# Three branch pairs of a recurrent stage: the wide form of a seven-product scheme in place of the narrow one

## The chip, the cores and the metric

The kernel runs on one core of a Trainium2 chip. The metric is device time in microseconds (us) of one execution, lower is better. The times before are those of three runs; the profile is of one more execution, taken by the hardware profiler.

## The reference

One hybrid decoder layer on 512 tokens of width 1024, in float32:

```python
f = swiglu(rms_norm(h, ...), ...);  h = h + 0.5 * rms_norm(f, ...)
u = rms_norm(h, mix_norm_pre);      proj = u @ w_in          # q, k, v, xr, yr, gl
attn_d = dilated_attention(q, k, v) @ w_attn_branch
rec    = rg_lru(conv4(xr)) * gelu(yr)                        # 1024 channels, 4 heads of 256
rec_d  = rec @ w_rec_branch
merged = sigmoid(gl)[0] * attn_d + sigmoid(gl)[1] * rec_d
h = h + rms_norm(merged @ w_out, ...)
f = swiglu(rms_norm(h, ...), ...);  h = h + 0.5 * rms_norm(f, ...)
```

The change touches `yr`, the "branch" of the recurrence: 1024 of the output columns of `w_in`, taken head by head as two blocks of 128 columns. For heads 0, 1 and 2 these products are computed by another sequence of instructions; what is computed is the same.

## The kernel before

**Precision.** Every float32 operand is kept as two parts, a high part rounded to the matmul's own format (fp32r) and a low part, the rest. A product is the sum of three matmuls: high weights with high input, high weights with low input, low weights with high input. `split` (L302, L303) makes the parts: ScalarE copies the high part, VectorE subtracts it to get the low one.

**Seven products for eight.** Two weight blocks of 128 columns ("g" and "u") and two halves of 256 tokens form a 2 x 2 product with 8 halves' products over 512 input rows each. The kernel uses a seven-product scheme: sums of weight blocks (`w_forms_within`, L704 on: additions L713 to L717 and four splits) and sums of input quarters (the forms `t`, made once for the whole stage) give products p1 to p7, and sums of these give the four outputs g[0], g[1], u[0], u[1] of 128 x 256. TensorE accumulates in PSUM tiles of 128 x 512 float32 ("acc", five buffers in turn, and "aux", three); a running sum goes from one buffer to another by a ScalarE copy, and the next product accumulates onto the copy.

There are two ways to run it:

- The **narrow** form, `seven_on` (L733): one product is, for each of four 128-row blocks of the input, three matmuls of 256 columns (`seventh`, L729 to L731), so 84 matmuls in a pair. It uses four "acc" buffers, half of each. Four results are moved with ScalarE copies of 256 columns (the copies b to y, z to c5, b to c6, b to v), two outputs are evicted by ScalarE and two by VectorE.
- The **wide** form, `seven_wide` (L762): high and low part of the input lie side by side, so one matmul of 512 columns (L779) multiplies the high weights with both, and one of 256 columns (L780) adds low weights times high input to the second half of the buffer. 56 matmuls in a pair. The two halves of a buffer are added only when a result leaves PSUM: `move` (L784) copies 512 columns, `fold` (L790, L791) is a ScalarE copy and a VectorE addition of 256 columns, `sum_of` (L797, L798) two VectorE additions. It uses five "acc" buffers, all of each.

The wide form is what the attention stage uses for its query and key pairs and for the four gate pairs, which end at about 600 us. The recurrent stage uses the narrow form for its four branch pairs, with the signs that the scheme leaves on u (`two_tiles`: scale -1 in the ScalarE eviction, a `scalar_tensor_tensor` on VectorE).

**The recurrent stage** (600 to 820 us) follows a list of steps:

```python
LRU_ORDER = (("branch", 0), ("branch", 1), ("conv", 0), ("branch", 2), ("gates", 0), ("conv", 1), ("branch", 3),
             ("gates", 1), ("conv", 2), ("gate1", 1), ("gates", 2), ("conv", 3), ("gate1", 2), ("gates", 3),
             ("gate1", 3))
```

`conv` is two blocks of 24 matmuls of 512 columns (L315 to L317) and, for each, a VectorE copy out of PSUM (L1559), a ScalarE scaling (L1560), three VectorE taps (L1562) and a split. `gates` multiplies the convolved columns ("rec", later "rb") with the gate weights of a head into "aux" and "acc" tiles; ScalarE applies the sigmoid (L1618) and `recur` runs the recurrence on ScalarE (L1629 to L1642, four activation tables) and VectorE (L1634 to L1647, with a scan). `gelus` (L1587) applies the GELU to the branch results of heads 0 and 1 after branch 1, and of heads 2 and 3 after branch 3. Each step's weights are split one step ahead.

**What sets the order.** Each engine runs its instructions in one order, which a planner writes when the program is built: it takes the program order, priorities (evictions are raised by `EVAC` = 200 places, weight preparation by `AHEAD` = 100) and its own cost estimates. So a change in one step can move instructions of other steps on an engine. TensorE, ScalarE (ACT) and VectorE (DVE) wait for each other by semaphores; the weights come as one stream of transfers on SyncE's queue (SP), and a few transfers on GpSimd's (POOL).

Of the kernel before, what the change touches and what calls it, by code (L numbers as in the profile page):

```python
# [12 lines left out]
AF = mybir.ActivationFunctionType  # L13
ALU = mybir.AluOpType
# [169 lines left out]
def hybrid_layer(ctx: ExitStack, tc: tile.TileContext, xT: bass.AP, xN: bass.AP, wst: bass.AP,  # L184
                 first: bass.AP, rows: bass.AP, consts: bass.AP, bias: bass.AP, out: bass.AP):
    nc = tc.nc
    DVE, ACT, PE = nc.vector, nc.scalar, nc.tensor
# [71 lines left out]
    def fetch(key, slot=None, ahead=0):  # L259

        with tc.high_priority(offset=ahead if slot else state["ahead"]):
            src = raw_of(key)
            w = src.shape[-1]
            t = slot() if slot else w8() if w > 512 else w4()
            split(t[:, 0, :w], t[:, 1, :w], src)
            return t[:, 0, :w], t[:, 1, :w]
# [38 lines left out]
    def acc_ps():  # L305
        return psum.tile([P, T], F32, name="acc", tag="acc", bufs=5)
# [4 lines left out]
    def tmp(name):  # L311
        return tpool.tile([P, T], F32, name=name, tag="t")
# [17 lines left out]
    def gemm(ps, wt, x, sl=slice(0, T), ks=None):  # L330
        n = x.n
        a, b = k128(wt[0], n), k128(wt[1], n)
        for k in ks or range(n):
            mm3(ps, a[:, k, :], b[:, k, :], x.hi[k][:, sl], x.lo[k][:, sl], k == 0, k == n - 1)
# [17 lines left out]
    HALVES = (slice(0, HB), slice(HB, T))  # L352
# [380 lines left out]
    def seven_on(t, w, g0, g1, u0, u1):  # L733

        b, z, y, v = (acc_ps()[:, :HB] for _ in range(4))

        def copy(ps, dst=None):
            if dst is None:  # L740
                dst = tpool.tile([P, HB], F32, name="c", tag="c", bufs=CB)
            with tc.high_priority(offset=EVAC):
                ACT.activation(dst, ps, AF.Copy)  # L743
            return dst

        seventh(t, w, "p1", b, True)
        copy(b, y)
        seventh(t, w, "p5", z, True)
        c5 = copy(z)
        seventh(t, w, "p6", b, False)  # L750
        c6 = copy(b)
        seventh(t, w, "p2", y, False)
        g0(y)
        seventh(t, w, "p7", b, False)
        copy(b, v)
        u1(b, c5)
        seventh(t, w, "p3", z, False)
        g1(z, c6)
        seventh(t, w, "p4", v, False)
        u0(v)  # L760

    def seven_wide(t, w, g, u, seen=lambda ap: ap, then=lambda: None):  # L762


        b, z, y, v, o = (acc_ps() for _ in range(5))

        def two(ps):
            return ps[:, :HB], ps[:, HB:]

        def product(p, ps, start):  # L770
            at = t[p].at
            part, cross = ps.rearrange("q (s c) -> q s c", s=2), two(ps)[1]
            if len(at(0, 0).shape) == 3:
                part = ps.rearrange("q (s b t) -> q s b t", s=2, b=2)
                cross = cross.rearrange("q (b t) -> q b t", b=2)
            for k in range(4):
                ks = slice(k * P, (k + 1) * P)
                wh, wl = w[p][:, 0, ks], w[p][:, 1, ks]
                PE.matmul(part, wh, at(BOTH, k), start=start and k == 0, stop=False, skip_group_check=True)  # L779
                PE.matmul(cross, wl, at(0, k), start=False, stop=k == 3, skip_group_check=True)  # L780

        def move(dst, src):
            with tc.high_priority(offset=EVAC):
                return ACT.activation(dst, src, AF.Copy).ins  # L784

        def fold(ps, dst=None):
            out = tpool.tile([P, HB], F32, name="c", tag="c", bufs=CB) if dst is None else dst
            x, y_ = two(ps) if dst is None else map(seen, two(ps))
            with tc.high_priority(offset=EVAC):
                ACT.activation(out, x, AF.Copy)  # L790
                DVE.tensor_add(out, y_, out)  # L791
            return out

        def sum_of(dst, ps, c):
            x, y_ = two(ps)
            with tc.high_priority(offset=EVAC):
                DVE.tensor_add(c, x, c)  # L797
                DVE.tensor_add(dst, seen(y_), seen(c))  # L798

        product("p1", b, True)  # L800
        move(y, b)
        product("p5", z, True)
        c5 = fold(z)
        product("p6", y, False)
        move(v, y)
        c6 = fold(y)
        product("p2", b, False)
        fold(b, g[0])
        product("p7", v, False)
        moved = move(o, v)  # L810
        sum_of(u[1], v, c5)
        with tc.issue_after(moved):
            then()
        product("p3", z, False)
        sum_of(g[1], z, c6)
        product("p4", o, False)
        fold(o, u[0])

    def seven(t, w, z, g, u):

# [297 lines left out]
    for k in range(KC):  # L1118
        wh, wl, raw = wts[k]
        if k == 0:  # L1120
# [3 lines left out]
            for sl in HALVES:  # L1124
                tail = ACT.activation(wh[:, sl], raw[:, sl], AF.Copy).ins
            DVE.scalar_tensor_tensor(u1.lo[0], z, col("g1a", 0), u1.hi[0].bitcast(F32),
                                     op0=ALU.mult, op1=ALU.subtract)
# [69 lines left out]
    with ExitStack() as mx:  # L1197
# [38 lines left out]
        def values_two(steps, then):  # L1236
# [78 lines left out]
            for j in range(2):  # L1315
# [4 lines left out]
        t, steps = forms_of(lambda i, j: Form(lambda s, k: um_t[2 * i + k // 2][:, s, k % 2, HALVES[j]]),  # L1320
                            apool, False, rec_half)
# [38 lines left out]
        scale = -1.0 / math.sqrt(P)  # L1360
# [128 lines left out]
        for c in range(0, KC, 2):  # L1489
            g, u = tmp("g"), tmp("u")  # L1490
            seven_wide(t, pair_of(("pair", 52 + c, 53 + c)), [g[:, h] for h in HALVES], [u[:, h] for h in HALVES],
                       then=gate)
# [3 lines left out]
        for c in range(KC):  # L1496
            ps = acc_ps()
# [5 lines left out]
    with ExitStack() as mx:  # L1503
# [26 lines left out]
        def two_tiles(w, g, u):  # L1530

            lo, hi = HALVES

            def up(dst, ps, sign):
                with tc.high_priority(offset=EVAC):
                    ACT.activation(dst[:, lo], ps, AF.Copy, scale=sign)

            def g1(ps, c):
                with tc.high_priority(offset=EVAC):
                    DVE.tensor_add(g[:, hi], ps, c)  # L1540

            def u1(ps, c):
                with tc.high_priority(offset=EVAC):
                    DVE.scalar_tensor_tensor(u[:, hi], ps, -1.0, c, op0=ALU.mult, op1=ALU.subtract)

            seven_on(t, w, lambda y: up(g, y, 1.0), g1, lambda v: up(u, v, -1.0), u1)
# [19 lines left out]
        gels, late = {}, []  # L1566

        def branch(hd):

            gels[hd] = []  # L1570
            if ("branch", hd) in PAIRED:
                w = paired.pop(("branch", hd))
                gels[hd] = [lpool.tile([P, T], F32, name="ge", tag="ge", bufs=8) for _ in range(2)]
                two_tiles(w, *gels[hd])
                return
            for c in (2 * hd, 2 * hd + 1):
                ps = acc_ps()
                gemm(ps, fetch(("in", 44 + c)), um)
                ge = lpool.tile([P, T], F32, name="ge", tag="ge", bufs=8)
                with tc.high_priority(offset=EVAC):  # L1580
                    DVE.tensor_copy(ge, ps)
                gels[hd].append(ge)
# [67 lines left out]
        for i, (what, hd) in enumerate(LRU_ORDER):  # L1650
# [9 lines left out]
            def then():  # L1660
                if i + 1 < len(LRU_ORDER):
                    prepare(LRU_ORDER[i + 1])
# [21 lines left out]
        for c in range(KC):  # L1684
            if c < 3:
                ps = pss[c]
            else:
                ps = acc_ps()
# [163 lines left out]
```

## Time and profile before

| | |
|---|---|
| median of 3 runs | 1212.2 us (1211.42 to 1212.27) |
| profiled execution | 1211.87 us, its span 1210.1 us |
| TensorE busy | 1199.2 us (99%) |
| VectorE busy | 1029.0 us (85%) |
| ScalarE busy | 832.4 us (69%) |
| mean granted TensorE clock | 0.998 |
| chain that ended last | TensorE 88%, VectorE 6%, ScalarE 3%, DMA 2% |

The span is the time from the first to the last instruction of the profile; the rest of the execution's time lies around it. Matmuls are pipelined: each row's duration is longer than the distance to the next start, and the distance is what a matmul costs in a stream. A row of a timeline shows start, duration, engine, line, operation, output and inputs, and in brackets the idle time before it with what ended it.

### The profile page before, as it was taken

The numbers are of one execution on the slowest core, as the hardware profiler recorded it, in microseconds if no ns is written. First come the engines' busy times: TensorE is split into PE (matmuls) and PEld (weight loads), VectorE is DVE, ScalarE is ACT, GpSimd is POOL, SyncE is SP. The second block draws the span as 40 slices with busy tenths as digits, with TensorE's granted clock in tenths as the row PEclk, the third lists the DMA queues.
The fourth block names the chain that finished last, engine by engine and source line by source line (L and its number), as shares of the span: only waits on it lengthen the run. The fifth ranks groups of instructions, "written<-read, shape, count | busy, mean of one in ns | idle before, by whom it ended". The sixth has DMA issues, their size and how long they took to land.

```text
span 1210.1 us, 18990 instructions
## 1 busy us (share of the span) xinstructions
PE 1199.2 (99%) x7306; PEld 1073.7 (89%) x7306; DVE 1029.0 (85%) x1608; ACT 832.4 (69%) x1447; POOL 26.1 (2%) x51
## 2 busy tenths in 40 slices
PE   9999999999999999999999999999999999999997
PEld 8899999999888889888889888888899999999996
DVE  7999888989689899999867899775799888888964
ACT  7566787887566576677735897834566687877763
POOL 0000000000011000000000000000100000000000
PEclk9999999999999999999999999999999999999999
DMA  7234343435625232222323432235443333343341
GB/s 266 87 97 140 114 138 116 133 118 157 243 109 145 70 114 79 88 96 70 126 77 111 145 135 87 87 110 186 148 137 117 123 121 125 121 130 115 123 174 70
DMA packets 45819, 149.78 MB, mean 124 GB/s; under 512 B 5152, under 2 KB 8608, under 8 KB 45728
## 3 DMA queue, kind: packets, MB, share of 16 engines
q1 hardware_dynamic: 38160, 131.09, 32.5%
q0 software_dynamic: 7280, 17.30, 4.2%
q8 instruction: 57, 0.93, 0.3%
q14 instruction: 34, 0.28, 0.1%
q10 hardware_dynamic: 288, 0.17, 0.0%
HBM read 138.06 MB, written 6.29 MB: 119 GB/s over the span
## 4 chain that ended last, share of the span: by engine, by line
PE 88%; DVE 6%; ACT 3%; DMA 2%; issue 1%; DVEq 0%
PE acc L729 9%; PE acc L731 9%; PE acc L730 9%; PE acc L779 8%; PE acc L315 7%; PE acc L317 7%; PE acc L316 7%; PE acc L780 4%; PE aux L1037 3%; PE aux L1038 3%; PE aux L1039 3%; DVE w L303 2%; DMA raw<-in_w 2%; PE acc L433 2%; PE acc L432 2%; PE acc L431 2%
## 5 line engine op out<-in xcount | busy, mean ns | idle before, releaser
L303 DVE TENSOR_TENSOR w<-raw,w 128x1024 fp32r<-128x1024 f32 (+1 forms) x272 | 297.4, 1098 | 36.2 <-ACT w L302 35.2
L302 ACT ACTIVATE w<-raw 128x1024 fp32r<-128x1024 f32 (+1 forms) x272 | 259.9, 959 | 89.4 <-PE acc L317 42.7
L729 PE MATMUL acc<-big,w 128*128 128x256 f32 x920 | 260.5, 283 | 0.0
L731 PE MATMUL acc<-big,w 128*128 128x256 f32 x920 | 260.3, 283 | 0.0
L730 PE MATMUL acc<-big,w 128*128 128x256 f32 x920 | 260.3, 283 | 0.0
L729 PEld LDWEIGHTS acc<-big,w 128*128 128x128 f32 x920 | 176.2, 192 | 1.9
L730 PEld LDWEIGHTS acc<-big,w 128*128 128x128 f32 x920 | 176.2, 192 | 1.7
L731 PEld LDWEIGHTS acc<-big,w 128*128 128x128 f32 x920 | 176.3, 192 | 0.0
L779 PE MATMUL acc<-big,w 128*128 128x512 f32 x320 | 115.0, 397 | 0.0
L780 PE MATMUL acc<-big,w 128*128 128x256 f32 x320 | 90.8, 284 | 0.0
L1037 PE MATMUL aux<-w,xf 128*128 128x512 f32 x224 | 87.5, 393 | 1.4 <-ACT w L302 0.9
L1038 PE MATMUL aux<-w,xf 128*128 128x512 f32 x224 | 87.5, 391 | 0.0
L1039 PE MATMUL aux<-w,xf 128*128 128x512 f32 x224 | 87.2, 389 | 0.0
L779 PEld LDWEIGHTS acc<-big,w 128*128 128x128 f32 x320 | 60.1, 188 | 13.2 <-ACT acc L784 0.2
L303 DVE TENSOR_TENSOR w<-s,w 128x1024 fp32r<-128x1024 f32 x51 | 62.2, 1220 | 3.2 <-ACT w L302 2.7
L780 PEld LDWEIGHTS acc<-big,w 128*128 128x128 f32 x320 | 60.4, 189 | 0.1
L315 PE MATMUL acc<-xf,w 128*128 128x512 f32 (+1 forms) x168 | 58.8, 352 | 0.0
L316 PE MATMUL acc<-xf,w 128*128 128x512 f32 (+1 forms) x168 | 58.6, 349 | 0.0
L317 PE MATMUL acc<-xf,w 128*128 128x512 f32 (+1 forms) x168 | 58.6, 349 | 0.0
L302 ACT ACTIVATE w<-s 128x1024 fp32r<-128x1024 f32 x51 | 53.9, 1057 | 6.2 <-PE acc L731 3.0
L743 ACT ACTIVATE c<-acc 128x256 f32<-128x256 f32 x74 | 28.2, 383 | 40.4 <-PE acc L731 40.2
L1037 PEld LDWEIGHTS aux<-w,xf 128*128 128x128 f32 x224 | 41.9, 188 | 10.2 <-ACT w L302 1.5
(453 smaller groups left out, 2934.2 us busy)
## 6 DMA issues: line engine op xcount, KB each, us to landing
raw<-in_w SPq DMA_DIRECT2D x232, 512.0 KB, 3.5
big<-xf POOLq DMA_DIRECT2D x6, 512.0 KB, 3.4
gains<-in_rows POOLq DMA_DIRECT2D x5, 512.0 KB, 5.4
h<-in_x SPq DMA_DIRECT2D x8, 256.0 KB, 5.3
h<-in_xn POOLq DMA_DIRECT2D x4, 512.0 KB, 6.0
kept_m<-h POOLq DMA_DIRECT2D x4, 512.0 KB, 2.9
vals<-in_w SPq DMA_DIRECT2D x4, 512.0 KB, 6.2
h<-kept_m POOLq DMA_DIRECT2D x4, 512.0 KB, 6.1
```

Source lines behind the costliest of these rows:

```text
L302: state["split"] = ACT.activation(dh, src, AF.Copy).ins
L303: state["low"] = DVE.tensor_sub(dl, src, dh.bitcast(F32)).ins
L315: PE.matmul(ps, wh, xh, start=first, stop=False)
L316: PE.matmul(ps, wh, xl, start=False, stop=False)
L317: PE.matmul(ps, wl, xh, start=False, stop=last)
L729: PE.matmul(ps, wh, xh, start=start and k == 0, stop=False, skip_group_check=True)
L730: PE.matmul(ps, wh, xl, start=False, stop=False, skip_group_check=True)
L731: PE.matmul(ps, wl, xh, start=False, stop=k == 3, skip_group_check=True)
L779: PE.matmul(part, wh, at(BOTH, k), start=start and k == 0, stop=False, skip_group_check=True)
L780: PE.matmul(cross, wl, at(0, k), start=False, stop=k == 3, skip_group_check=True)
L1037: PE.matmul(ps, xh, wh, start=first and j == 0, stop=False, skip_group_check=True)
L1038: PE.matmul(ps, xh, wl, start=False, stop=False, skip_group_check=True)
```

## The change

The branch pairs of heads 0, 1 and 2 call `seven_wide` in place of `two_tiles`; head 3 keeps the narrow form. `seven_wide` gets a parameter for the sign of u: with -1 the ScalarE copy of a fold and the last VectorE operation of `fold` and `sum_of` apply it. Every other call has sign 1 and the instructions it had.

```diff
-    def seven_wide(t, w, g, u, seen=lambda ap: ap, then=lambda: None):
+    def seven_wide(t, w, g, u, seen=lambda ap: ap, then=lambda: None, sign=1.0):
...
-        def fold(ps, dst=None):
+        def fold(ps, dst=None, sign=1.0):
...
-                ACT.activation(out, x, AF.Copy)
-                DVE.tensor_add(out, y_, out)
+                ACT.activation(out, x, AF.Copy, scale=sign)
+                if sign > 0:
+                    DVE.tensor_add(out, y_, out)
+                else:
+                    DVE.scalar_tensor_tensor(out, y_, sign, out, op0=ALU.mult, op1=ALU.add)
...
-        def sum_of(dst, ps, c):
+        def sum_of(dst, ps, c, sign=1.0):
...
-                DVE.tensor_add(dst, seen(y_), seen(c))
+                if sign > 0:
+                    DVE.tensor_add(dst, seen(y_), seen(c))
+                else:
+                    DVE.scalar_tensor_tensor(dst, y_, sign, c, op0=ALU.mult, op1=ALU.subtract)
...
-        sum_of(u[1], v, c5)
+        sum_of(u[1], v, c5, sign)
...
-        fold(o, u[0])
+        fold(o, u[0], sign)
...
-                two_tiles(w, *gels[hd])
+                if hd in (0, 1, 2):
+                    seven_wide(t, w, *([x[:, h] for h in HALVES] for x in gels[hd]), sign=-1.0)
+                else:
+                    two_tiles(w, *gels[hd])
```

## The prediction

> **What bounds the kernel now.** I read the page first (busy time and the chain), then the windows around the branch pairs, the waits of TensorE in the recurrent stage, and last the timelines of ScalarE (ACT) and VectorE (DVE) at each place where the changed order touches one of those waits. Two lines of the page say whose time this is:
>
> ```profile
> PE 1199.2 (99%) x7306; PEld 1073.7 (89%) x7306; DVE 1029.0 (85%) x1608; ACT 832.4 (69%) x1447; POOL 26.1 (2%) x51
> PEclk9999999999999999999999999999999999999999
> ```
>
> TensorE is busy 99% at full granted clock, so the change can only give time by shorter TensorE work or by removing TensorE's waits; it can take time only by making new ones. The second view is busy time by window: branch pair 0, pair 1, pair 2 (with four gate matmuls in it), the gates and convolution behind it, pair 3 (narrow in both kernels), then one wide pair of the gate stage, and last a stretch of a wide pair beside a fuller VectorE.
>
> ```profile
> 622.51:632.55 10.04, 10.04 (x85) 10.03 (x84) 6.04 (x8) 5.92 (x9) 0.00 (x0) 1.00 0.05 13
> 632.55:642.70 10.15, 10.15 (x86) 10.08 (x85) 6.35 (x9) 8.01 (x13) 0.00 (x0) 1.00 0.50 166
> 653.61:664.58 10.97, 10.97 (x89) 10.78 (x88) 10.25 (x15) 7.77 (x12) 0.00 (x0) 1.00 0.20 60
> 664.58:680.09 15.51, 15.51 (x70) 12.77 (x69) 10.50 (x14) 14.35 (x20) 0.00 (x0) 1.00 0.32 102
> 680.09:692.61 12.52, 11.02 (x88) 10.57 (x87) 12.52 (x20) 9.34 (x16) 2.16 (x4) 1.00 0.50 174
> 590.75:600.52 9.77, 9.77 (x58) 8.57 (x57) 6.80 (x12) 7.75 (x15) 0.00 (x0) 1.00 0.40 140
> 558.62:567.07 8.45, 8.45 (x51) 7.36 (x49) 7.91 (x16) 8.25 (x25) 0.00 (x0) 1.00 0.19 64
> ```
>
> Columns: stretch, its length, then busy time and count of PE, PE's weight loads, DVE, ACT, POOL, the clock, DMA. TensorE never stops in the pairs to be changed, while in pair 3's window it stands for 12.52 - 11.02 = 1.5 us. The third view, the waits between 600 and 820 us, names that as the only TensorE wait over 0.2 us of the stage:
>
> ```profile
> PE aux L315 <- ACT w L302: 1.5, 1, 1.5
> ```
>
> Its place on the timelines of TensorE and ScalarE:
>
> ```profile
> 681.41 0.28 PE L731 MATMUL acc<-big,w 128*128 128x256 f32 x1
> 683.19 0.73 PE L315 MATMUL aux<-rec,w 128*128 128x512 f32 x2 [1.50 <-ACT w L302]
> ...
> 679.63 0.63 ACT L1640 ACTIVATE th<-th 128x512 f32<-128x512 f32 x1 [0.83 <-DVE gt L1636]
> 681.56 0.63 ACT L302 ACTIVATE rec<-sig 128x512 fp32r<-128x512 f32 x1 [1.29 <-DVE sig L1562]
> 682.10 1.04 ACT L302 ACTIVATE w<-raw 128x1024 fp32r<-128x1024 f32 x1
> 683.04 0.80 ACT L1560 ACTIVATE sig<-xr,first 128x512 f32<-128x512 f32 x1
> 683.75 0.36 ACT L743 ACTIVATE acc<-acc 128x256 f32<-128x256 f32 x1
> ...
> 687.99 0.63 ACT L302 ACTIVATE rec<-sig 128x512 fp32r<-128x512 f32 x1 [0.50 <-DVE sig L1562]
> 688.79 1.05 ACT L302 ACTIVATE w<-raw 128x1024 fp32r<-128x1024 f32 x1
> 689.95 0.37 ACT L743 ACTIVATE acc<-acc 128x256 f32<-128x256 f32 x1
> ```
>
> After pair 3's first product come three gate matmuls of head 1, whose weights ScalarE splits only at 682.10, behind an operation that waited for VectorE. TensorE loses 683.19 - 681.41 - 0.12 = 1.66 us (0.12 is one narrow matmul's place, 10.04 / 84).
>
> **The change, part by part.** (1) Matmuls. Per pair 84 matmuls of 256 columns become 28 of 512 and 28 of 256: the same 21,504 columns, 28 instructions fewer, 84 in all. The price is in the windows: a wide pair in full is 9.77 us against 10.04. Beside a fuller VectorE (7.91 of 8.45 us) 24 wide steps took 8.45, so 28 take 9.86. Pairs 0 and 1 have VectorE busy 6 of 10 us, so 9.77; pair 2 has it 10.25 of 10.97, so 9.86 against 10.97 less four gate matmuls at 15.51 / 68 = 0.23 each (0.94 with their start), 10.03. Gain 0.27 + 0.27 + 0.17 = 0.71 us. Bounds: all three like the crowded stretch, 0.5; all like the quiet one, 0.8. The Trainium skill, "TensorE: Matmul & The Clock Gate", section "Wait — 56ns, not 53.3ns?", puts the fixed cost of a warm matmul at about 2.5 ns; by it, estimated from that page, 84 matmuls fewer are 0.2 us. The rows give 0.27 us / 28 = 9.6 ns, and the measurement decides.
>
> (2) Evacuation. The groups by shape:
>
> ```profile
> L784 ACT ACTIVATE acc<-acc 128x512 f32<-128x512 f32 x48 | 28.3, 589 | 11.0 <-PE acc L780 8.4 <-DVE e L1437 1.1 <-DVE xch L1415 1.1
> L743 ACT ACTIVATE acc<-acc 128x256 f32<-128x256 f32 x74 | 27.8, 376 | 3.6 <-PE acc L731 0.3
> L791 DVE TENSOR_TENSOR c<-acc,c 128x256 f32<-128x256 f32 x32 | 13.4, 420 | 4.0 <-ACT c L790 3.9
> L1587 ACT ACT_TABLE_LOAD x3 | 3.8, 1283 | 0.3 <-DVE ge L1540 0.3
> ```
>
> Per pair ScalarE gets three moves of 512 columns for two of 256 (3 x 0.589 - 2 x 0.376 = 1.0 us more; the four other copies keep their size), VectorE eight operations for two (6 x 0.42 = 2.5 us). In the order of instructions that the changed program has, three table loads fewer stand on ScalarE over the stage, 3 x 1.283 = 3.8 us less. All this is beside TensorE: it costs nothing while VectorE and ScalarE deliver in time. VectorE has 4 us free in pairs 0 and 1; in pair 2 only 10.97 - 10.25 = 0.72, so about 1.8 us of its 2.5 go into the next window, which has 15.51 - 10.50 = 5.0 free. Its next dense stretch begins with a convolution copy for which it stood idle 2.02 us, so the backlog should be gone by then:
>
> ```profile
> 674.86 1.09 DVE L1559 COPY xr<-acc 128x512 f32<-128x512 f32 x1 [2.02 <-PE acc L317]
> ```
>
> The order on SP's and POOL's queues is the same in both programs, so the weight stream is not moved past anything; no DMA is added.
>
> (3) Buffers. A wide pair holds all five "acc" buffers for four. They come round in turn: the pair's last one is written only at its sixth product, some 7 us after its start, and the convolution copies that free them come within 2 us of the convolution's end. No wait, bounds 0 to 0.3.
>
> (4) Pair 1 starts behind the GELU's table load. Today:
>
> ```profile
> 633.21 1.28 ACT L1587 ACT_TABLE_LOAD   x1
> 634.50 0.63 ACT L1587 ACTIVATE ge<-ge 128x512 f32<-128x512 f32 x1
> 635.04 0.37 ACT L743 ACTIVATE acc<-acc 128x256 f32<-128x256 f32 x1
> ...
> 635.46 0.39 PE L729 MATMUL acc<-rb,w 128*128 128x256 f32 x1
> ```
>
> The copy to "y" at 635.04 ends as the third product starts, which is 0.1 us late already (10.15 against 10.04). In the changed order load, first GELU and then pair 0's last fold (0.28 until the next starts) stand ahead of the 512-column move. TensorE ends pair 0 at 622.51 + 9.77 = 632.28 and its fold's copy must wait for the GELU: load 632.4, GELU 633.7, fold 634.2, move 634.5 to 635.1. The third product is due at 632.28 + 2 x 1.39 = 635.06. So 0.1 us again: no difference, bounds 0 to 0.5.
>
> (5) The gate matmuls of head 1. In the changed order the three stand behind pair 3 and all its products; ScalarE has split their weights long before. The 1.66 us go. What is late next are the copies inside pair 3, on a ScalarE that waits for VectorE's convolution chain. VectorE's spacings there, start to start (copy 0.91, short operation 0.60, weights 1.13, tap 0.66):
>
> ```profile
> 681.44 1.07 DVE L1559 COPY xr<-acc 128x512 f32<-128x512 f32 x1
> 682.35 0.69 DVE L1635 SCALAR_TENSOR_TENSOR r<-gt,r 128x512 f32<-128x512 f32 x1
> 682.95 0.68 DVE L303 TENSOR_TENSOR rec<-sig,rec 128x512 fp32r<-128x512 f32 x1
> 683.55 1.22 DVE L303 TENSOR_TENSOR w<-raw,w 128x1024 fp32r<-128x1024 f32 x1
> 684.68 0.75 DVE L1562 SCALAR_TENSOR_TENSOR sig<-xr,first,sig 128x512 f32<-128x512 f32 x1
> 685.34 0.69 DVE L1636 TENSOR_TENSOR gt<-th,r 128x512 f32<-128x512 f32 x1
> ```
>
> TensorE reaches the window of 664.58 at 663.8, pair 3 at 679.4 (0.7 earlier), its fourth product at 683.7 and the seventh, which accumulates onto the copied "v", at 679.4 + 6 x 1.44 = 688.0. On VectorE the first convolution copy moves from 674.86 to 674.1; in the changed order it opens seventeen operations that end with the second column's last tap: copy 0.92, four of 0.60, two weights 1.13, five taps 0.66, second copy 0.92, the low part 0.60, two more of 0.60, and the last tap 0.75: it ends near 686.4. ScalarE's split of that column then runs 686.7 to 687.3, a weight split to 688.2 (spacing 0.94, from 682.10 to 683.04), and the copy to "v" ends near 688.6: TensorE waits 0.6. Bounds: 0, if VectorE is 0.6 ahead of this; 1.66, if the old wait only moves. I take 0.6, since each spacing is a row's.
>
> (6) Gates of head 2. Today the low part of the second column is written from 716.56 and the first matmul that needs it, the fifth, starts at 720.15 (the other two rows: the stage's last low part and its reader):
>
> ```profile
> 716.56 0.69 DVE L303 TENSOR_TENSOR rb<-sig,rb 128x512 fp32r<-128x512 f32 x1
> 720.15 0.39 PE L316 MATMUL aux<-rb,w 128*128 128x512 f32 x1
> ...
> 785.75 0.69 DVE L303 TENSOR_TENSOR rb<-ge,rb 128x512 fp32r<-128x512 f32 x1 [0.70 <-ACT rb L302]
> 788.52 0.39 PE L316 MATMUL acc<-rb,w 128*128 128x512 f32 x1
> ```
>
> 716.56 + 0.69 leaves 2.9 us of cover. TensorE comes 1.8 earlier, and in the changed order two more operations of the recurrence (0.60 each) and a weight split (1.13 less the one it replaces) stand ahead of that low part, so the cover ends at about nothing: I take 0.15, bounds 0 and 1.5. Behind that, the order is the same from the branch product on, and the stage's last low part, the other pair of rows, has 788.52 - 786.44 = 2.1 us of cover and two of the table loads fewer ahead of it: nothing.
>
> Sum: 0.71 + 1.66 - 0.6 - 0.15 = 1.6 us less. The profiled execution took 1211.87 (span 1210.1 and 1.8 around it), the median is 1212.2, 0.3 above; so 1210.3 against the profiled one, 1210.6 as a median. A difference of 0.2% (2.4 us) is about what a measurement of this kernel can tell from no change, and 1.6 lies inside.
>
> **The rivals.** F, no new wait: VectorE is a little faster through its stretch and (5) and (6) cost nothing; 0.8 + 1.66 = 2.5 us, 1209.7. For it: ScalarE saves 3.8 us of table loads. Against: VectorE has no free microsecond in pair 3's window (12.52 of 12.52).
>
> N, the gain does not show: wide steps at the crowded price in all pairs (0.5) and the old wait reappearing at the copy to "v" in full (1.66 - 1.66); 1211.7. For it: that copy starts at 689.95, 0.2 us after the product that it follows (692.61 less two products of 1.44), so an earlier TensorE meets it.
>
> S, slower: VectorE's added work, 18 x 0.42 = 7.5 us, is not absorbed but runs into the dense stretch from 674 on, and ScalarE, in its order, holds the copies of pair 3 behind it. The gain of 2.4 us is eaten at a lag of 2.4 and the kernel is slower by over 0.2% from a lag of 4.8. With 6 of the 7.5 us: 3.6 us more, 1215.8. For it: the 1.29 us that ScalarE stood at 681.56 with a ready weight split behind it. That ScalarE and VectorE are strict queues is also what the Trainium skill says ("TensorE: Matmul & The Clock Gate", section "Architectural detail: the array is 16× 32×32, not 1× 128×128"); the trace agrees by that row. Against: 4 us free in each of pairs 0 and 1, 5.0 before 680.
>
> **How the numbers follow.** Forecast 0.44, own range 1209.8 to 1211.6 (the new waits from 0.1 to 1.6); F 0.25; N 0.16; S 0.15. Faster by over 0.2% is F, 0.25; within is the forecast and N, 0.60; slower is S, 0.15. The range from 1209.2 (F with a little left over) to 1214.0 (S at a lag of some 4 us) leaves out about 0.05 below and 0.12 above.
>
> **What would show it.** Wide pairs of 9.8 us in place of 10.04, VectorE 18 operations of 256 columns more, the wait "PE aux <- ACT w" gone, and a TensorE wait of about 0.6 before pair 3's last product or none. The prediction is wrong if a wait over 1.5 us stands anywhere between pair 1 and the gates of head 2, or if the wide pairs take over 10 us.

## The result, and the profile after

The changed kernel takes 1209.64 us (median of 12 runs, 1208.9 to 1210.18), the kernel before 1212.21 (12 runs, 1211.24 to 1213.14): a ratio of 0.9979 with a 95% interval of 0.9971 to 0.9986, 2.6 us less. The prediction was 1210.6 (1209.2 to 1214.0; the forecast's own range from 1209.8, so the median is 0.2 below that). The profiled execution took 1209.61 us, its span 1207.8, at a mean granted clock of 0.999.

The busy times on the page after:

```profile
PE 1198.6 (99%) x7222; PEld 1070.1 (89%) x7222; DVE 1033.3 (86%) x1626; ACT 831.8 (69%) x1447; POOL 26.1 (2%) x51
```

84 matmuls fewer and 18 VectorE operations more; ScalarE has the same count and 0.6 us less (before: 7306, 1608, 1447 and 832.4 us). TensorE's busy time fell by 0.6 us only, the span by 2.3: most of what went was standing still.

Busy time by window, with the columns of the prediction: pair 0, pair 1, pair 2 (four gate matmuls in it), the gates and convolution behind it, pair 3.

```profile
623.18:632.98 9.80, 9.80 (x57) 8.54 (x56) 7.04 (x13) 6.75 (x11) 0.00 (x0) 1.00 0.04 7
632.98:642.78 9.80, 9.80 (x59) 8.52 (x57) 8.22 (x15) 8.68 (x14) 0.00 (x0) 1.00 0.52 168
653.68:664.49 10.81, 10.81 (x62) 9.33 (x60) 9.19 (x15) 8.45 (x13) 0.00 (x0) 1.00 0.17 51
664.49:680.00 15.51, 15.51 (x71) 12.77 (x69) 13.07 (x21) 14.24 (x19) 0.00 (x0) 1.00 0.37 114
680.00:690.74 10.74, 10.36 (x86) 10.14 (x84) 10.74 (x17) 9.98 (x16) 2.16 (x4) 1.00 0.61 213
```

The pairs are 0.24, 0.35 and 0.16 us shorter than 10.04, 10.15 and 10.97. The window behind pair 2 is 15.51 as before, with VectorE at 13.07 of it in place of 10.50: that is where part of its added work went. Pair 3, narrow in both, has 1.78 us less; the three gate matmuls that stood in it (0.23 each) now follow it. The only TensorE wait over 0.2 us between 600 and 820 us is a new one:

```profile
PE acc L729 <- ACT acc L743: 0.4, 1, 0.4
```

Its place on the timeline (start, duration, engine, line, operation; in brackets the idle time before and what ended it): pair 3's seventh product on TensorE, ScalarE ahead of it, VectorE's copy of the second convolution, and at the gates of head 2 the low part that VectorE writes last, the first matmul and the fifth.

```profile
674.76 1.10 DVE L1565 COPY xr<-acc 128x512 f32<-128x512 f32 x1 [2.37 <-PE acc L317]
...
687.84 1.05 ACT L302 ACTIVATE w<-raw 128x1024 fp32r<-128x1024 f32 x1
688.79 0.37 ACT L743 ACTIVATE acc<-acc 128x256 f32<-128x256 f32 x1
...
688.56 0.28 PE L731 MATMUL acc<-big,w 128*128 128x256 f32 x1
689.22 0.39 PE L729 MATMUL acc<-rb,w 128*128 128x256 f32 x1 [0.38 <-ACT acc L743]
...
717.74 0.68 DVE L303 TENSOR_TENSOR rb<-sig,rb 128x512 fp32r<-128x512 f32 x1
718.00 0.40 PE L315 MATMUL aux<-rb,w 128*128 128x512 f32 x1
718.94 0.39 PE L316 MATMUL aux<-rb,w 128*128 128x512 f32 x1
```

The seventh product starts 689.22 - 688.56 = 0.66 us behind the last matmul of the sixth, where 0.12 is the usual distance: it waits for the copy to "v" that stands behind a weight split. From the first matmul of pair 0 to the first gate matmul of head 2 (this is "the stage" below) it is 718.00 - 623.18 = 94.82 us; before it was 719.21 - 622.51 = 96.70. So the stage gave 1.88 us. The rest lies elsewhere, and two other parts differ in length between the two profiled executions. The part ahead of pair 0 has the same instructions in both and took 0.67 us more after (pair 0 begins at 623.18 in place of 622.51); in the eleven traces of this case without an edit there it takes 622.42 to 623.48, so it varies by itself. The other is the end, from the layer norm of the last feed-forward block on (the first "aux<-w,xf" group behind 880 us to the start of the last matmul; "the last stage" below). That window before, and after:

```profile
919.94:1203.51 283.57, 282.20 (x1928) 262.44 (x1926) 231.61 (x322) 200.59 (x351) 2.66 (x5) 1.00 0.36 122
```

```profile
918.70:1201.25 282.55, 281.93 (x1928) 262.55 (x1926) 231.54 (x322) 200.80 (x351) 2.66 (x5) 1.00 0.37 122
```

The same instructions in the same order take 1.0 us less. With 1.88 in the stage, 0.67 against it ahead of it and 0.03 between the two stages, that is the 2.26 us between the two profiled executions. TensorE's waits from 880 us on, before:

```profile
PE aux L1037 <- ACT w L302: 0.9, 3, 0.5
PE aux L1037 <- ACT aux L1026: 0.5, 1, 0.5
```

and after (the line number is the same operation's):

```profile
PE aux L1043 <- ACT w L302: 0.6, 3, 0.2
```

The 0.5 us wait, at 1120 us, goes back by the chain of releases through ScalarE and VectorE to one weight transfer that landed late. The DMA view of before around its issue (queue, packets, MB, share of the engines; then the issue with KB and us to landing):

```profile
q8 instruction: 1, 0.02, 3.2%
q14 instruction: 1, 0.01, 0.6%
issues: line engine op xcount, KB each, median us to landing
raw<-in_w SPq DMA_DIRECT2D x1, 512.0 KB, 4.7
```

and of after around the same transfer:

```profile
q14 instruction: 1, 0.01, 0.6%
issues: line engine op xcount, KB each, median us to landing
raw<-in_w SPq DMA_DIRECT2D x1, 512.0 KB, 3.5
```

Before, a load of instructions on queue q8 runs beside it and it takes 4.7 us; after, the load is not there and it takes 3.5. The page of before counts these loads:

```profile
q8 instruction: 57, 0.93, 0.3%
```

2 x 7306 matmuls and weight loads in 57 loads are 256 instructions each: q8 brings TensorE's instructions, and where a load falls is fixed by how many instructions came earlier. The change takes out 168 of them. Whether that is a cause or a coincidence is what the later experiments ask.

### The profile page after: what moved, and what is told of

Same layout as the page of the kernel before. It is cut to its first block, busy times and chain, and to the rows that moved or that the text cites. A ratio compares the mean times of both kernels' runs of the same rounds, so it can differ in the third digit from the quotient of the medians.

```text
span 1207.8 us, 18850 instructions
## 1 busy us (share of the span) xinstructions
PE 1198.6 (99%) x7222; PEld 1070.1 (89%) x7222; DVE 1033.3 (86%) x1626; ACT 831.8 (69%) x1447; POOL 26.1 (2%) x51
## 4 chain that ended last, share of the span: by engine, by line
PE 92%; DVE 4%; DMA 2%; ACT 1%; issue 1%; DVEq 0%; ACTq 0%
PE acc L779 10%; PE acc L729 9%; PE acc L731 9%; PE acc L730 9%; PE acc L315 7%; PE acc L317 7%; PE acc L316 7%; PE acc L780 5%; PE aux L1043 4%; PE aux L1044 4%; PE aux L1045 4%; PE acc L433 2%; PE acc L432 2%; PE acc L431 2%; DVE w L303 2%; DMA raw<-in_w 2%
## 5 line engine op out<-in xcount | busy, mean ns | idle before, releaser
L729 PE MATMUL acc<-big,w 128*128 128x256 f32 x860 | 243.6, 283 | 0.0
L731 PE MATMUL acc<-big,w 128*128 128x256 f32 x860 | 243.4, 283 | 0.0
L730 PE MATMUL acc<-big,w 128*128 128x256 f32 x860 | 243.3, 283 | 0.0
L729 PEld LDWEIGHTS acc<-big,w 128*128 128x128 f32 x860 | 164.8, 192 | 1.8
L730 PEld LDWEIGHTS acc<-big,w 128*128 128x128 f32 x860 | 164.8, 192 | 1.5
L731 PEld LDWEIGHTS acc<-big,w 128*128 128x128 f32 x860 | 164.8, 192 | 0.0
L779 PE MATMUL acc<-big,w 128*128 128x512 f32 x380 | 136.5, 398 | 0.0
L780 PE MATMUL acc<-big,w 128*128 128x256 f32 x380 | 107.5, 283 | 0.0
L779 PEld LDWEIGHTS acc<-big,w 128*128 128x128 f32 x380 | 71.4, 188 | 16.0 <-ACT acc L784 0.2
L780 PEld LDWEIGHTS acc<-big,w 128*128 128x128 f32 x380 | 71.7, 189 | 0.3
L779 PE MATMUL acc<-rb,w 128*128 128x512 f32 x152 | 55.5, 397 | 0.0
```

The costliest lines, as they stand in the source:

```text
L729: PE.matmul(ps, wh, xh, start=start and k == 0, stop=False, skip_group_check=True)
L730: PE.matmul(ps, wh, xl, start=False, stop=False, skip_group_check=True)
L731: PE.matmul(ps, wl, xh, start=False, stop=k == 3, skip_group_check=True)
```

## The experiments

The first four kernels shared a chip with the kernel before (1211.82 us, median of 33 runs), the next four another (1212.23, 31 runs), the last four a third (1211.86, 13 runs). A stage's length is read from each one's trace.

**The kernel before, once more.** No edit.

> The kernel before, once more. The stage is taken from the first matmul of branch pair 0 to the first gate matmul of head 2: 719.21 - 622.51 = 96.70 us before, 718.00 - 623.18 = 94.82 after. Theory A (what the stage lost, 1.88 us, is the change; the rest of the difference of the two profiles, 0.4 us in it after 800 us and 0.7 against it before 600, varies from one execution to the next): this run has 96.7 in the stage, and its TensorE waits near 943 and 1120 us (0.62 and 0.65 us in the profile before) come out otherwise than in the first profile; ratio 1.000. Theory B (the second feed-forward runs better because the stage before it ends earlier): this run shows the same waits near 943 and 1120 us again, to 0.1 us.

1212.22 us (ratio 1.0, 0.9991 to 1.0009), the stage 96.70 to the hundredth, with the wait of 1.5 for the gate weights. The last stage took 283.70, with a wait of 0.9 at 1121 us, the place where the first trace of before has 0.5, and the transfer issued there landed in 5.0 us. The wait near 943 us did not return: it is 0.2 here, as in all the other traces, and 0.5 in the first. So each theory is half right: the stage repeats closely, one of the two late waits repeats, and the other was that execution's. The median stands 0.4 above that of the same kernel beside it: smaller differences between medians aren't read below.

**Heads 0 and 1 wide.**

```diff
-                if hd in (0, 1, 2):
+                if hd in (0, 1):
```

> Only the pairs of heads 0 and 1 get the wide form; in its order of instructions the three gate matmuls of head 1 stay where they were, inside pair 3, and the activation table loads stay 31. Theory A (two parts that add: 0.24 to 0.35 us for each wide pair, and 1.66 us for the moved gate matmuls less a new wait of 0.66): the wait of 1.5 us before the gate matmuls is there again, the stage takes 96.7 - 0.6 = 96.1 us, ratio 0.9995. Rival (the gain is all from the wide form, and the wait is filled by it): the stage takes 95.4 or less, ratio 0.9988 or less.

The windows of pairs 0 and 3 (columns as above):

```profile
622.86:632.66 9.80, 9.80 (x57) 8.54 (x56) 7.05 (x13) 6.75 (x11) 0.00 (x0) 1.00 0.04 9
...
679.83:692.36 12.53, 11.04 (x89) 10.58 (x87) 12.53 (x20) 9.33 (x16) 2.16 (x4) 1.00 0.50 172
```

The wide pairs alone give what was expected of them, a stage of 96.10, and pair 3 is untouched. The time did not follow: 1212.29 us, ratio 1.0004 (0.9995 to 1.0013). The trace shows where the 0.6 us went: the last stage took 284.21, 0.6 more than before.

**Head 2 wide alone.** The same line with `(2,)`.

> Only the pair of head 2 gets the wide form; the planner then writes the same new order behind it as in the changed kernel (gate matmuls of head 1 behind pair 3, 28 table loads). Theory A1 (the chain from the convolution's copy through VectorE's taps to ScalarE's copy in pair 3 hangs on TensorE, so the new wait of 0.66 us stays whatever pairs 0 and 1 take): gain 0.16 + 1.66 - 0.66 = 1.2 us, the stage takes 95.5, ratio 0.9990. Theory A2 (that chain runs at its own time, so a TensorE that comes 0.6 later waits 0.6 less): gain 1.8 us, the stage takes 94.9, ratio 0.9985, and the wait before pair 3's last product is 0.1.

Pair 3's window:

```profile
679.77:690.47 10.70, 10.31 (x86) 10.09 (x84) 10.70 (x17) 9.94 (x16) 2.16 (x4) 1.00 0.58 212
```

Stage 95.33, between the two expectations (95.5 and 94.9), with the gap before the seventh product at 0.67 us as in the changed kernel: the new wait comes with the new order, not with the wide pairs 0 and 1. 1210.89 us, ratio 0.9993 (0.9984 to 1.0002). Of the stage's gain, heads 0 and 1 are worth 0.60 us and head 2, with the order that it brings, 1.37.

**The gate matmuls moved, nothing wide.** In the kernel before they are held behind pair 3's last product; ScalarE and VectorE keep their order until past pair 3 (it first differs near 703 us).

```diff
-            PE.matmul(ps, wl, xh, start=False, stop=k == 3, skip_group_check=True)
+            state["last"] = PE.matmul(ps, wl, xh, start=False, stop=k == 3, skip_group_check=True).ins
...
+                        with tc.issue_after(state["last"]) if hd == 1 else nullcontext():
                           mm3(ps, a_[:, w, i, js]
...
```

> The kernel before, all pairs narrow, with one edit: the gate matmuls of head 1 are held behind pair 3's last product on TensorE. ScalarE's and VectorE's order inside pair 3 stay as before. Theory A (the gate wait is hidden only as far as the copies in pair 3 come in time, and in the order of before the copy to v ends near 690.1 while TensorE now reaches the last product at 688.6): the wait of 1.66 moves to pair 3's last product as about 1.5; gain 0.0 to 0.4 us, stage 96.3 to 96.7, ratio 0.9998. Rival (moving the three matmuls is worth the whole wait whatever the other engines do): no wait over 0.3, stage 95.0, ratio 0.9986.

TensorE's waits between 600 and 820 us:

```profile
PE acc L729 <- ACT acc L743: 1.0, 1, 1.0
PE acc L729 <- ACT c L743: 0.3, 1, 0.3
```

The stage took 96.73, the time 1212.0 (ratio 1.0, 0.9991 to 1.0009). With ScalarE in its old order the 1.5 us only changes hands, from the gate weights to pair 3's copies. It went somewhere else than the expectation said (mostly before the third product, not the seventh), but the point stands: moving the matmuls is worth nothing by itself. What the change gained there it gained because the program that it makes has another order on ScalarE and VectorE too. The last stage of this trace took 282.81 us. TensorE's instructions are as many as in the kernel before, and the transfer that landed in 4.7 and 5.0 us there took 4.2 and made no wait.

**The changed kernel, once more.** No edit.

> The changed kernel once more, on the chip of the other kernels of this group. The stage (first matmul of pair 0 to first gate matmul of head 2) took 94.82 us against 96.70 before, 1.88 less, and the pairs repeat to 0.05 us in every trace so far. Theory A, all of the gain is in the stage and what lies outside it varies from execution to execution: stage 94.8 again, the wait before pair 3's last product 0.66 again, ratio near 1 - 1.88 / 1212 = 0.9984. Theory B, something outside the stage gains too and does so in every execution: stage 94.8, ratio 0.9979 again, and the matmuls behind 820 us shorter by 0.5 us or more than before's in this trace too.

1209.56 us, ratio 0.9978 (0.9968 to 0.9987); stage 94.72, the gap before the seventh product 0.66 again. The last stage:

```profile
918.03:1200.77 282.74, 281.96 (x1928) 262.56 (x1926) 231.57 (x322) 200.60 (x351) 2.66 (x5) 1.00 0.37 122
```

Again 0.8 to 1.0 below the two traces of before, as theory B had it, but only 0.07 below the trace with the gate matmuls moved, whose last stage has before's instructions. And 0.9984, theory A's ratio, lies inside the interval of both measurements. So theory A isn't ruled out.

**Heads 0 and 1 wide, once more.**

> Only heads 0 and 1 wide, a second profile and timing of the same kernel. Its stage took 96.10, 0.60 less than before, but its median was 0.4 above the kernel before, and its trace lost 1.5 us to late weight transfers in the last stage (waits at 999, 1015, 1060 and 1076 us). Theory A, those late transfers are that execution's: stage 96.1 again, the waits in the last stage elsewhere or smaller, ratio 0.9995. Theory B, the shifted phase of the stage puts the last stage's transfers late every time: the same waits near 1015 and 1076 us, ratio 1.0004 or more.

1213.12 us, ratio 1.0006 (0.9997 to 1.0015): theory B. Stage 96.10 again, the last stage longer again, with the same waits:

```profile
919.51:1204.04 284.53, 282.37 (x1927) 262.42 (x1926) 231.16 (x322) 200.90 (x351) 2.67 (x5) 1.00 0.37 121
```

```profile
PE aux L1043 <- ACT w L302: 2.1, 3, 1.4
```

The longest follows a transfer issued at 1065.70, beside a load of TensorE's instructions (DMA view, as above):

```profile
q8 instruction: 1, 0.02, 3.0%
issues: line engine op xcount, KB each, median us to landing
raw<-in_w SPq DMA_DIRECT2D x1, 512.0 KB, 4.3
```

So three programs have, in two traces each, three lengths of a last stage whose instructions and order are the same (the trace with the gate matmuls moved, at 282.81, lies with the changed kernel's). What differs is the count of TensorE instructions ahead of it: the loads stand, counted from the "aux<-w,xf" group at 943.00 in before, at 111.5, 129.8, 150.5 and 167.2 us in before, at 106.3, 125.1, 141.5 and 161.5 after, and at 102.2, 123.5, 140 and 158 with heads 0 and 1 wide (each found in the DMA view to 0.25 us).

**ScalarE's weight split moved out of the way of the copy to "v".** In the changed kernel the split of the third convolution's first block is held behind that copy.

```diff
-                ACT.activation(dst, ps, AF.Copy)
+                state["moved"] = ACT.activation(dst, ps, AF.Copy).ins
...
-                ps, w = acc_ps(), fetch(("in", 36 + c))
+                with tc.issue_after(state["moved"]) if c == 4 else nullcontext():
+                    ps, w = acc_ps(), fetch(("in", 36 + c))
```

> The changed kernel with ScalarE's split of the weights of the third convolution's first block held behind pair 3's copy to v. In the changed kernel that split (687.84, 0.95 us to the next start) stands between the split of the second column and the copy to v (688.79), and TensorE waits 0.66 us for the copy. In the order of instructions of this kernel an operation of 0.6 us stands there instead. Theory A, the wait is for ScalarE's queue: the wait goes to about 0.3 (0.95 - 0.60 less), the stage to 94.5, ratio to the kernel before 0.0003 under that of the changed kernel. Rival, the copy waits for VectorE's chain however ScalarE is ordered: 0.66 stays, stage 94.8; or the held split makes the third convolution wait, up to 0.9 us, stage 95.0 to 95.4.

ScalarE there, with an operation of the recurrence in the split's place:

```profile
687.67 0.62 ACT L1652 ACTIVATE gt<-gt 128x512 f32<-128x512 f32 x1
688.19 0.37 ACT L743 ACTIVATE acc<-acc 128x256 f32<-128x256 f32 x1
```

The gap before the seventh product is 0.22 us (0.12 is the usual distance), a little better than expected, and the stage 94.39; a gap of 0.07 appeared in the gates of head 2. So the wait was for ScalarE's queue. 1209.33 us, ratio 0.9977 (0.9968 to 0.9985): 0.2 below the changed kernel on the same chip, which the measurement can't tell from nothing.

**Seven idle VectorE operations more in pair 2.** On a tile that nothing reads.

```diff
         c6 = fold(y)
+        if state.get("extra"):
+            with tc.high_priority(offset=EVAC):
+                spare_c = tpool.tile([P, HB], F32, name="c", tag="c", bufs=CB)
+                DVE.memset(spare_c, 0.0)
+                for _ in range(state["extra"]):
+                    DVE.tensor_add(spare_c, spare_c, spare_c)
```

> The changed kernel with seven idle VectorE operations more in pair 2 (a memset and six additions of 256 columns in a chain, 2.5 to 2.9 us by the 0.42 and its 0.34 spacing), on a tile that nothing reads. In the changed kernel VectorE stands idle 1.61 us for a transfer at 661.57 and 2.37 us for the second convolution at 674.76, 4.0 together. Theory A, VectorE's added work is free up to that idle time: pair 3's wait stays 0.66 (to 0.8), stage 94.8 to 95.0, ratio as the changed kernel's. Rival S, the added work runs into the dense stretch behind 674 and holds ScalarE's copies of pair 3: the wait grows by the 2.1 to 2.5 us of the additions, stage 97.0 or more, ratio 0.9998 to 1.0005.

Stage 94.76, the gap 0.66. VectorE's idle time before the second convolution's copy:

```profile
674.90 1.09 DVE L1571 COPY xr<-acc 128x512 f32<-128x512 f32 x1 [1.98 <-PE acc L317]
```

VectorE is busy 2.2 us more over the execution (1035.5 against 1033.3), and only 0.4 of it reached this point; the wait of 1.61 us for a weight transfer at 661.57 is gone, filled by the added work. So VectorE's work in pair 2 is free, with 2 us left over. 1210.31 us, ratio 0.9983 (0.9974 to 0.9992); the stage doesn't show the 0.75 against the changed kernel. Of the two profiled executions, 1.4 us apart, the difference is 0.61 in the last stage (283.35 against 282.74) and 0.76 ahead of pair 0.

**56 TensorE instructions more at the start of the changed kernel.** 14 more warm-up matmuls; the order behind them is the same on every engine but for one memset on VectorE.

```diff
-    for _ in range(WARM):
-        PE.matmul(wu[:, :P], ones, ones, start=True, stop=True)
+    for i in range(WARM + 14):
+        m = P if i < 4 else 1
+        PE.matmul(wu[:, :m], ones, ones[:, :m], start=True, stop=True)
```

> The changed kernel with 14 more warm-up matmuls at the start (of the 24, the first four of 128 columns as before, the others of one column), 56 TensorE instructions more ahead of the rest and the same order behind them on every engine. With heads 0 and 1 wide alone the program has just these 56 more than the changed kernel. Theory L, loads of TensorE's instructions (queue q8, one each 18 us or so, at a place that the count of instructions fixes) delay a weight transfer that is issued as they run, and the last stage's transfers that have no slack then hold TensorE: the loads that stand 106.3 and 125.1 us behind the last stage's first matmul (the first "aux<-w,xf" behind 880 us) in the changed kernel move to 102 and 123, as with heads 0 and 1 wide, the transfers issued there land in 4.0 to 4.4 us, and from that matmul to the last one it takes 283.8 to 284.5 us in place of 282.55 and 282.74; the time is 1.2 us or more above the changed kernel's beside what the start costs. Rival V, the last stage varies by itself: 282.5 to 283.4. The stage of the change stays 94.8 in both.

(The lengths of the last stage in this and the next two expectations are counted from the first "aux<-w,xf" group, the places of the loads from the third, as in the paragraph above.) The loads moved to 103.0 and 124.2 us, and the transfer issued at 101.8, 1.2 us ahead of the first, landed in 4.7 us (3.4 to 3.5 in the two traces of the changed kernel). The last stage and its waits:

```profile
926.00:1210.70 284.70, 282.50 (x1928) 262.35 (x1926) 231.22 (x322) 200.72 (x351) 2.67 (x5) 1.00 0.35 121
```

```profile
PE aux L1043 <- ACT w L302: 1.2, 3, 0.6
PE aux L1043 <- ACT aux L1032: 1.0, 2, 0.7
```

284.70 against 282.55 and 282.74, and a stage of 94.80: theory L, slightly above its upper end. The time is 1218.62, of which the longer start is 7.9 us (the first sum of squares begins at 32.75 in place of 25.12 and 24.59): 1210.7 without it, 1.1 above the changed kernel, where the expectation had 1.2 or more.

**200 TensorE instructions more at the start, heads 0 and 1 wide.** The same edit with 50 in place of 14: the loads should stand where the changed kernel has them.

> Heads 0 and 1 wide, with 50 more warm-up matmuls at the start (200 TensorE instructions; 56 less than the 256 of one load), so that the loads stand as in the changed kernel. The start may be up to 5 us longer; what is read is the part behind it. Theory L: loads near 106 and 125 us behind the last stage's first matmul in place of 102 and 123.5, and that stage 282.5 to 283.3 us in place of 284.21 and 284.53. Rival V, what makes the last stage long with heads 0 and 1 wide is not where the loads stand: 284 or more. The stage of the change 96.1 in both.

They do, at 106.3 and 125.3 us, and the last stage is short:

```profile
942.82:1225.45 282.63, 281.92 (x1928) 262.52 (x1926) 231.41 (x322) 200.87 (x351) 2.67 (x5) 1.00 0.36 122
```

```profile
PE aux L1043 <- ACT w L302: 0.7, 3, 0.3
```

1.6 and 1.9 us less than the two traces without the edit, with the stage at 96.10. The transfer that had landed in 4.3 us takes 3.5, and the next load comes 3 us behind its issue. The time is 1233.57 with a start 23.0 us longer: 1210.6 without it, against 1212.29 and 1213.12. Theory L.

**88 TensorE instructions more at the start of the kernel before.** The same edit with 22.

> The kernel before with 22 more warm-up matmuls at the start (88 TensorE instructions; with the 168 that the change takes out, one load of 256), so that the loads stand as in the changed kernel. Theory L: the load that stands 167.2 us behind the last stage's first matmul moves to 161 or 162; the transfer issued at 166.4, which landed in 4.7, 5.0 and 4.2 us in the three traces with that order, lands in 3.5, TensorE's wait of 0.65 and 1.02 us near 1120 us goes, and the last stage takes 282.5 to 283.1 us in place of 283.57, 283.70 and 282.81. Rival V: 283.3 or more, or the transfer lands late all the same. The stage of the change is 96.70 in both.

The load moved from 167.2 to 161.5 us. The last stage, and the transfer issued at 166.45:

```profile
930.66:1213.17 282.51, 281.90 (x1927) 262.49 (x1926) 231.42 (x322) 201.17 (x351) 2.67 (x5) 1.00 0.36 122
```

```profile
issues: line engine op xcount, KB each, median us to landing
raw<-in_w SPq DMA_DIRECT2D x1, 512.0 KB, 3.4
```

For the transfer and the wait this is theory L: 3.4 us in place of 4.7, 5.0 and 4.2, and no wait near 1120 us. The last stage is 1.1 us shorter than the first trace of before, but only 0.3 shorter than the trace with the gate matmuls moved, which lies in theory L's range with the loads where they were; so its length doesn't tell the theories apart. Nor do the times: 1222.57 less a start that is 10.7 longer is 1211.8, the same as before's 1211.86; the four runs go from 1221.54, which is the profiled one, to 1223.16.

**All four pairs wide.** The line with `(0, 1, 2, 3)`.

> All four branch pairs wide: in pair 3 too 28 matmuls fewer, six VectorE operations of 256 columns more (2.5 us) and ScalarE's 1.0 us; in its order one of head 1's gate matmuls stands inside pair 3. In pair 3's window VectorE has no free time (12.52 of 12.52 us before). Theory A, this is where rival S's price falls due: pair 3 and the gate matmul hold 2 us or more of waits (0.66 with the narrow pair), the stage 96.0 to 98.0 in place of 94.8, ratio 0.9990 to 1.0005. Rival, the work is absorbed here too: the stage 94.4 to 94.8, ratio under 0.9980.

Pair 3's window, now with one gate matmul in it, and ScalarE's copy onto which its fifth product accumulates:

```profile
679.99:690.48 10.49, 10.34 (x58) 8.75 (x57) 10.49 (x18) 10.19 (x16) 2.17 (x4) 1.00 0.59 209
```

```profile
685.29 0.59 ACT L784 ACTIVATE acc<-acc 128x512 f32<-128x512 f32 x1
```

Theory A falls. VectorE is busy for the whole window here too, and TensorE loses only 0.4 us in it (the fifth product begins 0.42 us behind the fourth's last matmul in place of 0.12, and its second matmul is 0.1 late); the stage is 94.31, the shortest of all the kernels run. By these rows the copies that TensorE waits for come early enough in this program's order, though VectorE has more to do; no run tests that order by itself. It has 31 table loads, as the kernel before, where the changed kernel has 28: a short stage doesn't need fewer of them. 1209.17 us, ratio 0.9977 (0.9968 to 0.9987): no faster than the changed kernel by what can be measured.

## Why the prediction was right, and where not

The sum was 1.6 us; the stage gave 1.88 and 1.98, and the whole kernel 2.6. The time came out at rival F's number, but not by F's mechanism: F has no new wait, and the new wait is there. That the median lies so close to F's 1209.7 is luck, since 0.7 us of the 2.6 come from outside the stage, where the prediction had nothing.

(1) Matmuls, 0.71 predicted: pairs 0, 1 and 2 gave 0.24 + 0.35 + 0.16 = 0.75, at 9.80, 9.80 and 9.87 us (10.81 less 0.94) for 9.77, 9.77 and 9.86. 28 instructions fewer are worth 0.24 us, 8.6 ns each. The Trainium skill ("TensorE: Matmul & The Clock Gate", section "Wait — 56ns, not 53.3ns?") has a fixed cost of about 2.5 ns, which these pairs don't bear out.

(2) Evacuation at nothing: right, with more room than was claimed. VectorE's idle time before the second convolution's copy, the point by which the backlog had to be gone, is 2.37 us with the added work, 2.02 without; seven operations more in pair 2 leave it at 1.98.

(3) No wait for a buffer: the only TensorE wait over 0.2 us in the stage is for the copy to "v".

(4) The third product of pair 1 still 0.1 late: wrong by that much. Pair 1 is as short as pair 0, the late start went from 0.11 to 0.04.

(5) The gate matmuls: the 1.66 us went, and the new wait of 0.6 came, where it was put, at the copy to "v" behind the weight split, with 0.66 - 0.12 = 0.54 us. The copy was to end near 688.6, which is 689.3 with the 0.67 us by which this trace comes later to pair 0; it ended at 688.79 + 0.37 = 689.16. The run in which only the matmuls moved shows that this term needed the new order of ScalarE and VectorE: reading that order operation by operation was what made it come out.

(6) Gates of head 2, 0.15: 0. The low part is written by 717.74 + 0.68 = 718.42, and the fifth matmul, which needs it, starts at 718.94 in its turn: 0.5 us of cover were left, where the prediction had about nothing. (This matmul lies behind the end of the stage as it is measured above.)

Rival N (the old wait returns in full) is what happened with the matmuls alone moved, not in the changed kernel. Rival S's added work did move into the window behind pair 2 (VectorE 13.07 us in place of 10.50), but its cover was larger than even the forecast said: neither 2.2 us more in pair 2 nor the wide pair 3 with no free VectorE time brought its price.

What the prediction had wrong isn't in the sum: "Behind that, the order is the same from the branch product on", which it counted as nothing. The order is the same, the time isn't always. Fewer TensorE instructions move every later load of TensorE's instructions against the weight stream. That this is worth 2 us at the worst place tried is shown by the two runs that moved the loads there and away (284.70 against 282.55 and 282.74, and 282.63 against 284.21 and 284.53). That it is also the 0.7 us by which the kernel gained more than its stage is not shown. The three traces with before's loads have a last stage of 283.57, 283.70 and 282.81 us; the four of the changed kernel and its near relatives, with the loads in the same places, have 282.55, 282.74, 283.05 and 283.35. The two groups overlap, the kernel before with moved loads had no better time, and 0.7 is within the measurement's interval. So where the 0.7 us come from stays open.

## What to carry to other kernels

Where an engine is full to 99%, count the waits that the new order of all engines makes and removes, not only the instructions saved: here more than half of the stage's gain was one wait, and moving the waiting instructions by themselves gave nothing. An edit that changes the number of instructions on the busiest engine also moves its instruction loads; if a later stage waits for its weight transfers, a microsecond or two can come or go there, as here, so compare stage by stage before believing that a part of the edit was worth nothing. A dummy edit at the start that moves the loads tells the two apart in the trace, stage by stage. It does so less well in the time, because the start that has to be taken off varies itself (by 1.1 us up to pair 0 here).

## What the runs showed of the hardware

A load of 256 TensorE instructions (14,612 of them in 57 loads before) comes each 15 to 26 us in the last stage. The 512 KB weight transfers whose lateness is followed above were issued at the same time as a load or up to 1.2 us ahead of one and landed in 4.0 to 5.0 us, where the same transfers away from a load took 3.4 to 3.7. TensorE's waits name no load, but with the loads moved the last stage took 284.70 us against 282.55, through the transfers. The Trainium skill, "Runtime: NRT & Kernel Launch", section "Instruction fetch mechanics", gives the block as 256 instructions and calls its cost mostly hidden. The traces agree on the size; on the cost they agree only for a load that meets no transfer that TensorE needs.

Not every overlap does harm: in the changed kernel a transfer issued at 161.1 us, 0.4 ahead of a load, landed in 3.5, and with all four pairs wide one issued at 166.9 beside a load at 166.5 in 3.4. How far ahead of the load the transfer is issued tells most of it. All 14 traces together, each of these transfers from 20 us ahead of the last stage on compared with the median of the same transfer in the traces where no load begins from 1 us before its issue to 2.5 us after it (transfers with fewer than four such traces left out):

| the load begins | transfers | over 0.25 us longer |
|---|---|---|
| 1.5 to 0.2 us before the issue | 35 | 5 |
| 0.2 us before to 0.6 after | 57 | 33 |
| 0.6 to 2.2 us after | 43 | 42 (median of all 43: 0.8 longer) |
| 2.5 to 3.6 us after | 81 | 9 |

In the second row it varies from one execution to the next. With the loads in the changed kernel's places one transfer is issued within 0.4 us of a load's start; in six traces it landed in 3.5 to 4.0 us, and the last stage took 282.51 to 282.63 us in the three with 3.5 or 3.6, 282.74 to 283.35 in the others.

The warm-up matmuls at the start cost the same with one column as with 128. Rows by shape in the run with 14 more of them, with 40 passes of one column and 8 of 128:

```profile
L1121 PE MATMUL aux<-ones 128*128 128x1 f32 x40 | 8.5, 348 | 0.0
L1121 PE MATMUL aux<-ones 128*128 128x128 f32 x8 | 2.1, 441 | 1.1 <-DVE eps L228 1.1
```

48 of them took from 1.05 to 11.31 us, 0.214 us each, as the 20 of 128 columns in the changed kernel did (1.05 to 5.35): 14 matmuls that were meant to cost next to nothing put the first product off by 6.0 us. Each pass loads 128 x 128 weights in both cases, which may be its price; no run here tests it.
